# Decode states read in place, B projected second, and the group norm one projection later in a hybrid pool/SSD trunk

## The chip, the core and the metric

The kernel runs on one core of a Trainium2 chip. The metric is the time of one execution on the device, in microseconds (us). Below, PE is TensorE (matmuls), PEld its weight loads, DVE is VectorE, ACT ScalarE, POOL GpSimd, and SP the engine whose queue issues the weight loads. All inputs and outputs are in the chip's main memory, and everything counts that the program does between its first and its last instruction.

## The reference

One layer of a streaming encoder is run for 256 new frames of one stream (the prompt) and 16 frames of each of 8 running streams (the sample), 384 columns in all, which share the weights. The input is normed and projected by `w_in`; the projection's columns are split into a pooling branch, z, xBC, dt and gates. The part that matters here is the state-space branch (SSD): 8 groups, each with 8 heads of 64 channels, one B and one C of 128 states.

```
xbc, new_conv = causal_conv(xbc, st_conv, p['conv_w'], p['conv_b'])   # 4 taps, SiLU
...
def step(h, inp):
    ...
    cb = jnp.einsum('btgn,bsgn->btsg', Cc, Bc)
    xdt = xc * dtc[..., None]
    y = jnp.einsum('btsgr,bsgrp->btgrp', cb[..., None] * decay, xdt)
    y = y + jnp.einsum('btgn,bgrpn->btgrp', Cc, h) * jnp.exp(cum)[..., None]
    last = cum[:, -1]
    w_end = jnp.exp(last[:, None] - cum)
    h = h * jnp.exp(last)[..., None, None] + jnp.einsum('bsgn,bsgr,bsgrp->bgrpn', Bc, w_end, xdt)
    return h, y
...
y = y + p['d_skip'].astype(jnp.float32).reshape(SSD_GROUPS, HEADS_PER_GROUP)[..., None] * xh
a_ssd = gated_rmsnorm(y.reshape(b, L, D_INNER), z, p['ssd_norm']).astype(u.dtype)
```

`gated_rmsnorm` multiplies y by silu(z) and norms it over each group of 512 channels. For the sample, every stream has 16 frames, so its new state h is its old one times a decay, plus the product of B and the weighted x over its own 16 frames. This last product, for 8 streams at once, is what the kernel calls `su`. The pooling branch, the gates, the two branch projections, `w_out`, and an MLP of 8192 channels with its norms follow the same input and make up the rest of the time.

## The kernel before

All matmuls of the projections are made of three passes of a reduced fp32 kind: each operand is split into a high part (a rounded copy) and a low part (the rest), and high times high, high times low and low times high are summed (`mm3`, lines 98 to 100). Weights are streamed in pieces of 512 KB, half a projection each: SP's queue loads a piece (`wfetch`, line 63), ACT copies the high part (`wh`, line 70), DVE subtracts it for the low part (`wl`, line 71). There are three buffers of each, and `take` keeps three split halves ahead of TensorE.

The part that the change touches is the loop over the groups, from about 418 to 1180 us. In each of its passes TensorE runs ten projections of 128 channels, each of two halves of 24 matmuls over 384 columns: x0, x1, B, C, x2, x3 and then z0 to z3. Two lumps of small matmuls stand between them. One comes in the middle, after x2, and finishes the second pair of heads of the group before (`prev`): its prompt states `t_pp` (line 696), then `t_cb` (line 652, C times B of the new group), `t_yT` and `t_Y` (line 682, the outputs), `t_yi` (line 661) and `t_su` (line 820). The other comes at the end, after z3, and does the same, without `t_cb`, for the first pair of the group itself; the profile has the first rows of both lumps as `py L696`.

What feeds them: `conv` (four taps and SiLU) on DVE and ACT makes x, B and C; `turned` turns x and B over (a transpose in blocks on DVE, four POOL DMAs to the scratch t_scr, a fifth that loads it back as xT or Bt). `xside` makes xdt and splits the weighted x into `xhl`; `bside` splits Bt into `Bhl`; `eside` makes the decay matrices E (Relu and Exp on ACT, a product with `cbm` on DVE); `dside` multiplies the loaded states hs with their decay. Work that consists of several DMAs is laid out over half projections by `steps` and `tick`.

For `t_su`, frames of the 8 streams lie on 128 partitions, 16 each. A stream's own 16 rows are not a unit that TensorE can address, so the low and the high half of B and x are stacked: b_scr and x_scr are written out and read back by 16 rows at a time (`leave` and `come`, lines 714 to 719 and 765 to 774) as `bst` and `xst`, each with 64 rows for one stream.

After the lump `final` adds the D skip, multiplies with z, squares (`ysq`, line 857 on ACT) and sums the squares into `ssum` (line 858 on POOL). `finish` is the group norm of the group before: `norm_bc` copies ssum's high part (`nh`, line 192, ACT), subtracts (`nl`, line 193, DVE), sums over partitions by two matmuls with ones (`bc_g`, lines 196 and 197), and `newton` (lines 182 to 186, DVE) takes the inverse root. Then DVE multiplies the four tiles zs (line 865), and POOL writes them out to a_scr. In the code `finish(prev)` stands ahead of `zproj(2)`.

A scheduler orders each engine's instructions once, when the program is built; on the chip each engine and each queue works in that order and waits at the instruction whose inputs are missing. Two kinds of functions on ACT, Silu on one side and Exp on the other, need different tables, and each switch is an ACT_TABLE_LOAD.

## Time and profile before

| what | value |
|---|---|
| median of 3 runs | 2664.36 us (2659.24 to 2667.16) |
| the profiled execution's own time | 2661.4 us |
| its span, first to last instruction | 2659.6 us |
| PE busy | 2638.4 us |
| DVE, ACT, POOL busy | 1521.6, 1169.5, 379.4 us |
| mean granted TensorE clock | 0.996 |
| main memory read, written | 414.97 MB, 49.58 MB |

The busy times say how long each engine had an instruction running. TensorE's matmuls are pipelined, so that a matmul's shown duration (0.33 us in the projections) is about twice the distance to the next one (0.16 us). The chain of work that ended last is followed backwards from the last instruction, at each step to what released it. Where TensorE waits for nothing, the chain runs along TensorE alone; where another engine or a DMA stands in it, TensorE had to wait, and the lines ahead of such a place show for what. A row of the chain has its start, its length and what it is. A row of waits has the engine and line that waited, what it waited for, and the total, the number and the longest of these waits in us.

### The profile page before, as it was taken

The numbers are of one execution on the slowest core, as the hardware profiler recorded it, in microseconds if no ns is written. First come the engines' busy times: TensorE is split into PE (matmuls) and PEld (weight loads), VectorE is DVE, ScalarE is ACT, GpSimd is POOL, SyncE is SP. The second block draws the span as 40 slices with busy tenths as digits, with TensorE's granted clock in tenths as the row PEclk, the third lists the DMA queues.
The fourth block names the chain that finished last, engine by engine and source line by source line (L and its number), as shares of the span: only waits on it lengthen the run. The fifth ranks groups of instructions, "written<-read, shape, count | busy, mean of one in ns | idle before, by whom it ended". The sixth has DMA issues, their size and how long they took to land.

```text
span 2659.6 us, 38491 instructions
## 1 busy us (share of the span) xinstructions
PE 2638.4 (99%) x15149; PEld 2457.0 (92%) x15149; DVE 1521.6 (57%) x2148; ACT 1169.5 (44%) x1820; POOL 379.4 (14%) x550
## 2 busy tenths in 40 slices
PE   9999999999999999999999999999999999999998
PEld 8998889999999999988888889999999999989897
DVE  7585335788888879756344346534444444444446
ACT  6443225566566757545322235433333333323233
POOL 0000002355454453530000000000000000000000
PEclk9999999999999999999999999999999999999999
DMA  7544446677777677767544544444444444444443
GB/s 273 154 134 152 147 148 232 202 232 225 244 240 240 227 237 248 222 213 250 173 158 151 189 162 136 139 138 137 136 135 135 135 135 135 135 135 136 136 137 130
DMA packets 144117, 467.09 MB, mean 176 GB/s; under 512 B 20864, under 2 KB 35776, under 8 KB 138944
## 3 DMA queue, kind: packets, MB, share of 16 engines
q1 hardware_dynamic: 112000, 365.76, 41.8%
q0 software_dynamic: 25024, 84.19, 9.4%
q10 hardware_dynamic: 6912, 14.68, 1.8%
q8 instruction: 119, 1.95, 0.3%
q14 instruction: 62, 0.51, 0.1%
HBM read 414.97 MB, written 49.58 MB: 175 GB/s over the span
## 4 chain that ended last, share of the span: by engine, by line
PE 93%; DVE 2%; ACT 2%; DMA 2%; issue 1%; POOL 0%; SPq 0%; DVEq 0%; ACTq 0%; POOLq 0%
PE pj_up L98 6%; PE pj_up L100 6%; PE pj_up L99 6%; PE wd L151 6%; PE wd L149 6%; PE wd L150 6%; PE pj_x L98 4%; PE pj_x L99 4%; PE pj_x L100 4%; PE pj_sp L150 3%; PE pj_sp L149 3%; PE pj_sp L151 3%; PE pj_z L100 3%; PE pj_z L99 3%; PE pj_z L98 3%; PE pj_gb L149 2%
## 5 line engine op out<-in xcount | busy, mean ns | idle before, releaser
L98 PE MATMUL pj_up<-x1h,wh_up 128*128 128x384 f32 (+1 forms) x1024 | 333.7, 326 | 0.0
L99 PE MATMUL pj_up<-x1l,wh_up 128*128 128x384 f32 (+1 forms) x1024 | 333.4, 326 | 0.0
L100 PE MATMUL pj_up<-x1h,wl_up 128*128 128x384 f32 (+1 forms) x1024 | 333.4, 326 | 0.0
L71 DVE TENSOR_TENSOR wl_wd<-w_wd,wh_wd 128x1024 fp32r<-128x1024 f32 x126 | 154.4, 1225 | 240.3 <-ACT wh_wd L70 240.3
L149 PE MATMUL wd<-wh_wd,hh 128*128 128x512 f32 x756 | 286.5, 379 | 0.0
L150 PE MATMUL wd<-wl_wd,hh 128*128 128x512 f32 x756 | 286.5, 379 | 0.0
L151 PE MATMUL wd<-wh_wd,hl 128*128 128x512 f32 x756 | 286.5, 379 | 0.0
L70 ACT ACTIVATE wh_wd<-w_wd 128x1024 fp32r<-128x1024 f32 x126 | 133.1, 1057 | 322.2 <-PE wd L151 261.7
L70 ACT ACTIVATE wh_up<-w_up 128x1024 fp32r<-128x1024 f32 x126 | 133.1, 1057 | 292.8 <-PE pj_up L99 229.4
L71 DVE TENSOR_TENSOR wl_up<-w_up,wh_up 128x1024 fp32r<-128x1024 f32 x126 | 154.4, 1225 | 178.8 <-ACT wh_up L70 178.5
L98 PE MATMUL pj_x<-xgh,wh_x 128*128 128x384 f32 x768 | 251.9, 328 | 0.0
L99 PE MATMUL pj_x<-xgl,wh_x 128*128 128x384 f32 x768 | 250.4, 326 | 0.0
L100 PE MATMUL pj_x<-xgh,wl_x 128*128 128x384 f32 x768 | 250.4, 326 | 0.0
L99 PEld LDWEIGHTS pj_up<-x1l,wh_up 128*128 128x128 f32 x1024 | 193.6, 189 | 0.2
L98 PEld LDWEIGHTS pj_up<-x1h,wh_up 128*128 128x128 f32 x1024 | 193.6, 189 | 0.2
L100 PEld LDWEIGHTS pj_up<-x1h,wl_up 128*128 128x128 f32 x1024 | 193.6, 189 | 0.0
L98 PE MATMUL pj_z<-xgh,wh_z 128*128 128x384 f32 x512 | 170.0, 332 | 1.9 <-ACT wh_z L70 1.9
L100 PE MATMUL pj_z<-xgh,wl_z 128*128 128x384 f32 x512 | 170.2, 332 | 0.9 <-DVE wl_z L71 0.9
L99 PE MATMUL pj_z<-xgl,wh_z 128*128 128x384 f32 x512 | 169.9, 332 | 0.0
L71 DVE TENSOR_TENSOR wl_sp<-w_sp,wh_sp 128x1024 fp32r<-128x1024 f32 x64 | 78.4, 1225 | 154.0 <-ACT wh_sp L70 154.0
L151 PEld LDWEIGHTS wd<-wh_wd,hl 128*128 128x128 f32 x756 | 142.9, 189 | 20.3
L150 PEld LDWEIGHTS wd<-wl_wd,hh 128*128 128x128 f32 x756 | 142.9, 189 | 20.1
(336 smaller groups left out, 6119.3 us busy)
## 6 DMA issues: line engine op xcount, KB each, us to landing
w_up<-w_up SPq DMA_DIRECT2D x128, 512.0 KB, 3.3
w_wd<-w_down SPq DMA_DIRECT2D x128, 512.0 KB, 3.3
w_x<-w_in SPq DMA_DIRECT2D x96, 512.0 KB, 4.6
w_z<-w_in SPq DMA_DIRECT2D x64, 512.0 KB, 4.1
w_sp<-w_ssd SPq DMA_DIRECT2D x64, 512.0 KB, 3.3
w_ga<-w_ga SPq DMA_DIRECT2D x32, 512.0 KB, 3.4
w_pp<-w_pp SPq DMA_DIRECT2D x32, 512.0 KB, 3.3
hs<-ssm POOLq DMA_DIRECT2D x16, 1024.0 KB, 6.9
```

The source lines that it names most:

```text
L70: cut[0] = s.activation(h, w, AF.Copy)
L71: cut[1] = v.tensor_tensor(l, w, h.bitcast(F32), ALU.subtract)
L98: te.matmul(out, wh, xh, start=first, stop=False, **how)
L99: te.matmul(out, wh, xl, start=False, stop=False, **how)
L100: return te.matmul(out, wl, xh, start=False, stop=last, **how)
L149: te.matmul(out, mh, vh, start=k == 0, stop=False)
L150: te.matmul(out, mh, vl, start=False, stop=False)
L151: last[0] = te.matmul(out, ml, vh, start=False, stop=k == nk - 1)
```

## The change

The states of the streams are computed from `xhl` and B where they lie. `t_su` uses row tiles of 32 partitions, two streams each. To keep two streams apart, B is multiplied beforehand with a mask that is one on the 16 rows of the even (or odd) streams and zero on the others (`Bm`, two ACT copies with a scale per partition, the mask in two new columns of `vec`). There are then 4 row tiles, 2 parities and 3 passes of high and low parts, 24 matmuls instead of 8, in four PSUM tiles at once. The scratch tensors b_scr and x_scr, the tiles bst and xst, and all their DMAs are gone.

The order of the projections is x0, B, x1, C, x2, x3, with the weights stored accordingly. `finish(prev)` stands behind `zproj(2)`. The tiles zs have 8 buffers instead of 7, and ysq two instead of one.

```
@@
-        bst = []
-        for i in range(2):
-            bst.append(pd1.tile([P, 4, P], F32R, name=f"bst{i}"))
@@ def bside(D)
-            bscr = b_scr[D.g]
-            D.bs = bst[D.g % 2]
-
-            def leave():
-                gp.dma_start(bscr, D.Bhl[:, :, 2, :].bitcast(F32))
-
-            def come():
-                for p4 in range(4):
-                    for h2 in range(2):
-                        gp.dma_start(
-                            D.bs[h2 * 64 + p4 * 16 : h2 * 64 + p4 * 16 + 16].bitcast(F32),
-                            bscr.rearrange("(q h r) l n -> h l r q n", q=4, h=2)[h2, p4 // 2],
-                        )
-
-            steps.append([leave] + [lambda: None] * 2 + [come])
+            D.Bm = pd.tile([P, 2, 2, P], F32R, tag="Bm", name=f"Bm{D.g}", bufs=1)
+            for h in range(2):
+                s.activation(
+                    D.Bm[:, h],
+                    D.Bhl[:, :, 2, :].bitcast(F32),
+                    AF.Copy,
+                    scale=vec[:, V_PAR + h : V_PAR + h + 1],
+                )
@@ def xside(S)
-            xscr = x_scr[S.qd]
-            def leave():
-                sy.dma_start(
...
-            def come():
-                S.xst = pd.tile([P, 4, 2 * P], F32R, tag="xst", name=f"xst{S.nm}", bufs=1)
-                for p4 in range(4):
-                    for h2 in range(2):
-                        gp.dma_start(
...
-            if S.qd == 2 * G - 1:
-                leave()
-                come()
-            else:
-                steps.append([leave] + [lambda: None] * 3 + [come])
@@ def state(S), t_su
-                for r2 in (0, 2):
-                    su = [sstile(f"su{S.nm}_{r2}_{h}") for h in range(2)]
-                    for r in range(2):
-                        for h in range(2):
-                            t = slice(h * 64, h * 64 + 64)
+                su = [sstile(f"su{S.nm}_{q}") for q in range(4)]
+                for h in range(2):
+                    for n, (bl, xl) in enumerate(((0, 0), (0, 1), (1, 0))):
+                        for q in range(4):
+                            t = slice(q * 32, q * 32 + 32)
                             i = te.matmul(
-                                pairs(su[h][:, r * 256 : r * 256 + 256]),
-                                S.D.bs[t, r2 + r, :],
-                                woven(S.xst[t, r2 + r, :]),
-                                start=True,
-                                stop=True,
+                                pairs(su[q][:, h * 256 : h * 256 + 256]),
+                                S.D.Bm[t, h, bl, :],
+                                S.xhl[t, xl, :, 2, :].rearrange("p j n -> p n j"),
+                                start=n == 0,
+                                stop=n == 2,
                             )
@@ def final(S)
-                    qs = pd.tile([P, T], F32, tag="ysq", name=f"ysq{g}_{j}", bufs=1)
+                    qs = pd.tile([P, T], F32, tag="ysq", name=f"ysq{g}_{j}")
@@ the loop
-            cs = [g * 4, g * 4 + 1, 32 + g, 40 + g, g * 4 + 2, g * 4 + 3]
+            cs = [g * 4, 32 + g, g * 4 + 1, 40 + g, g * 4 + 2, g * 4 + 3]
@@
-                z = pd.tile([P, T], F32, tag="zs", name=f"zs{g}_{j}", bufs=7)
+                z = pd.tile([P, T], F32, tag="zs", name=f"zs{g}_{j}", bufs=8)
@@
+            zproj(2)
             if g:
                 finish(prev)
-            zproj(2)
             dside(S)
             zproj(3)
```

How the orders differ at the places that matter is shown for group 4 and its turn to group 5. First TensorE, where the projections of z follow each other. Before, the norm's two matmuls stand between z1 and z2:

```order
L98 MATMUL pj_z_1_8397<-xgh_514,wh_z_1_1_8348 128x384
L99 MATMUL pj_z_1_8397<-xgl_515,wh_z_1_1_8348 128x384
L100 MATMUL pj_z_1_8397<-xgh_514,wl_z_1_1_8349 128x384
L196 MATMUL bc_g_8489<-nh_g_8485,onesr 128x384
L197 MATMUL bc_g_8489<-nl_g_8486,onesr 128x384
L98 MATMUL pj_z_2_8513<-xgh_250,wh_z_2_0_8400 128x384
L99 MATMUL pj_z_2_8513<-xgl_251,wh_z_2_0_8400 128x384
```

Now, between z2 and z3:

```order
L98 MATMUL pj_z_2_8467<-xgh_490,wh_z_2_1_8433 128x384
L99 MATMUL pj_z_2_8467<-xgl_491,wh_z_2_1_8433 128x384
L100 MATMUL pj_z_2_8467<-xgh_490,wl_z_2_1_8434 128x384
L196 MATMUL bc_g_8535<-nh_g_8531,onesr 128x384
L197 MATMUL bc_g_8535<-nl_g_8532,onesr 128x384
L98 MATMUL pj_z_3_8560<-xgh_226,wh_z_3_0_8470 128x384
```

The norm has moved by a whole projection on TensorE.

Next ACT, from the split of z1's second half (wh_z_1_1) to that of z2's first (wh_z_2_0). L792, L790, L800 and L801 make E, L601 is the SiLU of a conv, L954 that of z0, nh_g is the norm's copy, the DMA rows load the decays for E. Before:

```order
L70 ACTIVATE wh_z_1_1_8348<-w_z_1_1_8346 128x1024
L792 ACTIVATE E_0_8298<-cbc_0_1_7874,tok 128x128 x3
L800 ACTIVATE E_0_8298<-E_0_8298 128x2x128
L801 ACTIVATE E_0_8298<-E_0_8298 128x2x256
L646 DMA cbc_1_0_8393<-cum_scr 128x768
L601 ACT_TABLE_LOAD
L601 ACTIVATE xs_8293<-cacc_8288,vec 128x384
L954 ACTIVATE zs_0_8379<-zs_0_8379 128x384
L646 DMA cbc_1_1_8395<-cum_scr 128x768
L70 ACTIVATE wh_z_2_0_8400<-w_z_2_0_8398 128x1024
L70 ACTIVATE wh_z_2_1_8443<-w_z_2_1_8441 128x1024
L192 ACTIVATE nh_g_8485<-ssum_7682 128x384
```

Now (L758, L756, L766 and L767 make E, L596 is the conv's SiLU, L919 that of z0):

```order
L758 ACTIVATE E_0_8298<-cbc_0_1_7866,tok 128x128 x3
L766 ACTIVATE E_0_8298<-E_0_8298 128x2x128
L70 ACTIVATE wh_z_1_1_8347<-w_z_1_1_8345 128x1024
L596 ACT_TABLE_LOAD
L596 ACTIVATE xs_8290<-cacc_8285,vec 128x384
L767 ACT_TABLE_LOAD
L767 ACTIVATE E_0_8298<-E_0_8298 128x2x256
L641 DMA cbc_1_0_8392<-cum_scr 128x768
L919 ACT_TABLE_LOAD
L919 ACTIVATE zs_0_8378<-zs_0_8378 128x384
L641 DMA cbc_1_1_8394<-cum_scr 128x768
L70 ACTIVATE wh_z_2_0_8399<-w_z_2_0_8397 128x1024
```

The part of E that stood behind wh_z_1_1 has moved ahead of it, and between the two splits there are three table loads instead of one.

Last DVE, around the end lump, before from the last of the norm's four multiplications on: wl_x is the low half of the x and B weights (x_0 and x_1 are the halves of a projection; the last one in the second pair of lists is the second half of the second projection), L953 and L918 multiply the projection of z, L865 and L830 are the norm's multiplications of zs, L844 and L809 the D skip, L852 and L817 the product with z, L829 and L794 the addition of su, L753 and L741 make xdt and weight xT.

```order
L865 SCALAR_TENSOR_TENSOR zs_3_7614<-zs_3_7614,vec,ny_g_8494 128x384
L71 TENSOR_TENSOR wl_x_0_8582<-w_x_0_8579,wh_x_0_8581 128x1024
L71 TENSOR_TENSOR wl_x_1_8612<-w_x_1_8609,wh_x_1_8611 128x1024
L953 TENSOR_TENSOR zs_3_8639<-pj_z_3_8578,rstd 128x384
L71 TENSOR_TENSOR wl_x_0_8720<-w_x_0_8717,wh_x_0_8719 128x1024
L844 SCALAR_TENSOR_TENSOR xs_7762<-xs_7762,vec,Y_0_0_8649 128x384
L852 TENSOR_TENSOR zs_0_8379<-zs_0_8379,xs_7762 128x384
L844 SCALAR_TENSOR_TENSOR xs_7859<-xs_7859,vec,Y_0_1_8651 128x384
L753 TENSOR_TENSOR xdt_1_8789<-xT_1_8218,tok 128x384
L741 TENSOR_TENSOR yis_1_8685<-py_1_8642,tok 128x256
L829 TENSOR_TENSOR hs_0_7957<-hs_0_7957,su_0_0_0_8687 128x2x256
L829 TENSOR_TENSOR hs_0_7957<-hs_0_7957,su_0_0_1_8688 128x2x256
```

Now, from z3's own multiplication on:

```order
L918 TENSOR_TENSOR zs_3_8621<-pj_z_3_8560,rstd 128x384
L830 SCALAR_TENSOR_TENSOR zs_0_7347<-zs_0_7347,vec,ny_g_8540 128x384
L830 SCALAR_TENSOR_TENSOR zs_1_7431<-zs_1_7431,vec,ny_g_8540 128x384
L830 SCALAR_TENSOR_TENSOR zs_2_7497<-zs_2_7497,vec,ny_g_8540 128x384
L830 SCALAR_TENSOR_TENSOR zs_3_7590<-zs_3_7590,vec,ny_g_8540 128x384
L809 SCALAR_TENSOR_TENSOR xs_7754<-xs_7754,vec,Y_0_0_8631 128x384
L809 SCALAR_TENSOR_TENSOR xs_7950<-xs_7950,vec,Y_0_1_8633 128x384
L817 TENSOR_TENSOR zs_0_8378<-zs_0_8378,xs_7754 128x384
L729 TENSOR_TENSOR yis_1_8667<-py_1_8624,tok 128x256
L817 TENSOR_TENSOR zs_1_8462<-zs_1_8462,xs_7950 128x384
L71 TENSOR_TENSOR wl_x_0_8718<-w_x_0_8715,wh_x_0_8717 128x1024
L741 TENSOR_TENSOR xdt_1_8787<-xT_1_8216,tok 128x384
```

And the rows ahead of the second half's split itself, before:

```order
L852 TENSOR_TENSOR zs_1_8480<-zs_1_8480,xs_7859 128x384
L753 TENSOR_TENSOR xT_1_8218<-xT_1_8218,tok 128x384
L753 TENSOR_TENSOR xdt_1_8789<-xT_1_8218,tok 128x384
L805 TENSOR_TENSOR hs_1_8483<-hs_1_8483,decb 128x2048
L71 TENSOR_TENSOR wl_x_1_8750<-w_x_1_8747,wh_x_1_8749 128x1024
L753 TENSOR_TENSOR xT_1_8218<-xT_1_8218,tok 128x384
L802 TENSOR_TENSOR E_1_8798<-E_1_8798,cbm_8169 128x1024
```

and now:

```order
L741 TENSOR_TENSOR xT_1_8216<-xT_1_8216,tok 128x384
L741 TENSOR_TENSOR xdt_1_8787<-xT_1_8216,tok 128x384
L768 TENSOR_TENSOR E_1_8796<-E_1_8796,cbm_8151 128x1024
L741 TENSOR_TENSOR xT_1_8216<-xT_1_8216,tok 128x384
L771 TENSOR_TENSOR hs_1_8465<-hs_1_8465,decb 128x2048
L71 TENSOR_TENSOR wl_x_1_8748<-w_x_1_8745,wh_x_1_8747 128x1024
L749 TENSOR_TENSOR xhl_1_8792<-xT_1_8216,xhl_1_8792 128x768
```

The four multiplications of zs have moved behind the multiplication of z3 (L953, L918), the first half's split from ahead of the D skip to behind the products with z, and the E product and a second xT product (L753, L741) from behind the second half's split to ahead of it.

More of the change, by code (lines that the diff above doesn't have):

```diff
@@ L30 @@
 C_RC, C_SCAN, C_END = 1032, 1096, 1504
-V_GPRE, V_GMLP, V_PSC, V_CW, V_CB, V_NRM, V_DSK, V_DTB, V_ALOG, V_END = 0, 16, 32, 48, 240, 288, 320, 352, 353, 384
+V_GPRE, V_GMLP, V_PSC, V_CW, V_CB, V_NRM, V_DSK, V_DTB, V_ALOG, V_PAR, V_END = 0, 16, 32, 48, 240, 288, 320, 352, 353, 354, 384
 def build(ctx, tc, io):
@@ L206, in build @@
     gb_scr = [dram.tile([P, 3, 512], F32, name=f"gb_scr{i}") for i in range(4)]
-    b_scr = [dram.tile([P, 2, P], F32, name=f"b_scr{i}") for i in range(G)]
-    x_scr = [dram.tile([P, 2, 2, P], F32, name=f"x_scr{i}") for i in range(16)]
     t_scr = [dram.tile([T, P], F32, name=f"t_scr{i}") for i in range(40)]
@@ L912, in build @@
                 eside(prev.p[1], 0)
-            D.xs.append(conv(u0 + 1, g * 4 + 1, "xs", 6))
-            xturned(D, g, 1)
+            D.BT = conv(u0 + 1, 32 + g, "BT", 2)
+            D.Bt = pd.tile([P, 3, P], F32, tag="Bt", name=f"Bt{g}", bufs=1)
+            turned(D.BT, 32 + g, D.Bt)
             if g:
@@ L917, in build @@
             cload(D.p[0])
-            D.BT = conv(u0 + 2, 32 + g, "BT", 2)
-            D.Bt = pd.tile([P, 3, P], F32, tag="Bt", name=f"Bt{g}", bufs=1)
-            turned(D.BT, 32 + g, D.Bt)
+            D.xs.append(conv(u0 + 2, g * 4 + 1, "xs", 6))
+            xturned(D, g, 1)
             pload(D.p[0])
@@ L1421 @@
     for g in range(G):
-        cols += [6144 + (g * 4 + j) * P for j in range(2)]
-        cols += [6144 + 4096 + g * P, 6144 + 5120 + g * P]
+        cols += [6144 + g * 4 * P, 6144 + 4096 + g * P, 6144 + (g * 4 + 1) * P, 6144 + 5120 + g * P]
         cols += [6144 + (g * 4 + j) * P for j in range(2, 4)]
@@ L1437 @@
     vec[:NH, V_ALOG] = a["a_log"][0]
+    for h in range(2):
+        vec[:, V_PAR + h] = (np.arange(P) // TS_) % 2 == h
     d = {
```

13 lines of the change are left out of this document (3 added, 10 removed).

## The prediction

> **What bounds the kernel now.** I read the busy times first, then the chain that ended last, then the waits of the engine that carries it.
>
> ```profile
> PE 2638.4 (99%) x15149; PEld 2457.0 (92%) x15149; DVE 1521.6 (57%) x2148; ACT 1169.5 (44%) x1820; POOL 379.4 (14%) x550
> ...
> PE 93%; DVE 2%; ACT 2%; DMA 2%; issue 1%; POOL 0%; SPq 0%; DVEq 0%; ACTq 0%; POOLq 0%
> ```
>
> TensorE is the bound. The change can win only by closing holes in its work (the 7% of the chain that is not PE), and lose by adding matmuls or opening new holes. All removed DMAs and scalar work count at nothing unless they stand ahead of such a hole. So the next view is the waits of TensorE (us in total, times, longest):
>
> ```profile
> PE bc_g L196 <- ACT nh_g L192: 3.6, 2, 2.0
> PE bc_g L197 <- DVE nl_g L193: 2.7, 3, 0.9
> PE pj_z L98 <- ACT wh_z L70: 1.9, 1, 1.9
> ...
> PE cb L652 <- ACT xs L601: 0.9, 1, 0.9
> ```
>
> Nearly all lies in the loop over eight groups, and most of it at the group norm's broadcast matmuls (bc_g), the step that the change moves. How much time that costs is read from the chain, in which every pass of the loop shows the first matmuls of its two lumps of small matmuls (start, us):
>
> ```profile
> 499.85 0.67 PE py L696 x6
> ...
> 589.41 0.67 PE py L696 x6
> ...
> 632.90 0.67 PE py L696 x6
> ...
> 678.34 0.67 PE py L696 x6
> ...
> 772.70 0.67 PE py L696 x6
> ...
> 816.20 0.67 PE py L696 x6
> ...
> 820.73 0.64 PE su L820 x8
> ...
> 860.90 0.67 PE py L696 x6
> ...
> 864.56 0.64 PE su L820 x8
> ...
> 904.40 0.67 PE py L696 x6
> ...
> 953.73 0.67 PE py L696 x6
> ...
> 1041.93 0.67 PE py L696 x6
> ...
> 1136.61 0.67 PE py L696 x6
> ```
>
> The rows alternate between the lump in a group's middle and the one at its end. From an end to the next middle it is 43.50 (772.70 to 816.20, 860.90 to 904.40), from a middle to its end 44.70 (816.20 to 860.90), a whole group 88.20. Against that, group 1 (499.85 to 589.41) has 1.36 too much, the second half of group 2 (632.90 to 678.34) 0.74, group 3 (678.34 to 772.70) 6.16, the second half of group 5 (904.40 to 953.73) 4.63, group 7 (1041.93 to 1136.61) 6.48. Sum 19.4 us. With the 0.9 that the first group's cb matmuls wait, the loop holds about 20.3 us of loss. Its mechanism in group 7, in the chain:
>
> ```profile
> 1104.95 9.68 DMA w_z<-w_in
> ...
> 1114.71 1.06 ACT wh_z L70
> ...
> 1117.55 0.69 PE bc_g L197
> 1118.23 0.32 PE pj_z L98
> ```
>
> The DMA part of the page has the usual landing beside it (KB each, median us):
>
> ```profile
> w_z<-w_in SPq DMA_DIRECT2D x64, 512.0 KB, 4.1
> ```
>
> So a weight load takes 9.68 us where 4.1 is usual, its split wh_z stands on ScalarE ahead of the norm's copy nh, and TensorE waits at bc_g although the weights that come behind bc_g would be there in time. Then each projection matmul advances by 0.32 instead of 0.16 us: the granted clock has fallen, as the stretches show (stretch, length, busy times, clock, DMA share, GB/s):
>
> ```profile
> 816.00:861.00 45.00, 45.00 (x333) 43.80 (x332) 39.88 (x61) 29.37 (x54) 22.71 (x36) 1.00 0.74 240
> 1085.40:1136.60 51.20, 48.29 (x331) 46.56 (x330) 39.93 (x60) 29.02 (x52) 27.68 (x37) 0.93 0.69 222
> ```
>
> A clock of 0.93 over 51.2 us is 3.6 us, so a hole of some 2 to 3 us costs as much again in clock; the wait of 0.9 at cb is not followed by such matmuls. The Trainium skill ("TensorE: Matmul & The Clock Gate", section "Why this matters for your kernels") allows holes up to about 3 us before the clock halves; this trace halves it after less, so the rows decide. By the page, the price of rival C below would be 7 x 2.2 = 15 us, and it would end at 2663 instead.
>
> Group 3 has another cause:
>
> ```profile
> 730.30 6.04 POOL ssum L858
> ...
> 739.85 0.96 ACT wh_z L70
> ...
> 742.11 0.69 PE pj_z L100
> 742.80 0.32 PE pj_z L98
> ```
>
> ScalarE's second square ysq has one buffer and must wait until GpSimd's addition (6.04 us here) has read the first one; behind it on ScalarE stands the split of z0's second half, for which TensorE waits at 740.
>
> **The change, part by part.**
>
> Norm one projection later, and second ysq buffer. bc_g now stands between z2 and z3, 7.8 us later, while nh stands on ScalarE right behind the split of z2's second half, which TensorE wants 3.9 us earlier than bc_g. In groups 5 and 7 nh was 2.0 late at most: 7.8 covers it. The price is that newton and the four multiplications of zs fall 7.8 us later on VectorE, at the group's end (below). With two ysq buffers group 3's wait is gone. I take all 20.3; the bounds are 14 (group 3's 6.2 stays, from the GpSimd addition or another cause) and 20.3.
>
> States. Before, 8 matmuls of 64 rows, in four rounds of two tiles side by side:
>
> ```profile
> L820 PE MATMUL su<-xst,bst x128: 272/272/374, 503.4 to 1175.3; 64*128 64x256 f32 x128
> ...
> 1045.52 0.71 PE L820 MATMUL su<-xst,bst 64*128 64x256 f32 x8
> ```
>
> 0.71 is the first round's 0.374 and three more of 0.112. Now 24 matmuls of 32 rows, with as many columns. If four tiles run side by side, these are six rounds: 2 x 0.112 = 0.22 more, x16 pairs = +3.6 us, all on TensorE. No row shows four row tiles at once. If only two run together, it is 12 rounds, 0.90 more, +14.3 in all; if none do, 24 rounds, 2.24 more, +36. It cannot be under four rounds. I take +3.6, nearest to the su row, where tiles do run together and the rounds go by columns. The four sums need four PSUM banks at once instead of two and two; VectorE adds the same four halves of hs (L829), so that side costs nothing.
>
> Scratch trips. SP loses 16 x_scr issues, which wait long:
>
> ```profile
> SPq L765 <- DVE xhl L761: 118.4, 16, 16.5
> ```
>
> and the weight loads queue behind them, while GpSimd's queue loses 25 issues per group (16 xst, 8 bst, b_scr). The turned x3, the state load hs and a_scr now start sooner there. I count no gain of its own: where TensorE did not wait, these were hidden. The hs load (1024 KB), however, now always stands early, ahead of the late z weights, as it did before only in groups 1, 3, 5 and 7; that is rival E. The two Bm copies (128x256) cost ScalarE less each than the 0.53 of the 128x384 zs row below, at the beginning of a group's second half, and are wanted only by the su at its end, 35 us later: nothing.
>
> B second. x1's turned tile arrives a projection later, and is first read by VectorE in the second half of the group; Bt has more time than before, which frees ScalarE's Bhl. No cost on TensorE; in the first group the cb wait goes with it.
>
> New tight places. The scheduler's order on ScalarE now switches between Silu and Exp three times between the splits of z1's and z2's halves, where there was one such load:
>
> ```profile
> 837.52 1.28 ACT L601 ACT_TABLE_LOAD   x1
> ...
> 840.18 0.53 ACT L954 ACTIVATE zs<-zs 128x384 f32<-128x384 f32 x1 [0.74 <-DVE zs L953]
> 840.61 2.10 ACT L70 ACTIVATE wh_z<-w_z 128x1024 fp32r<-128x1024 f32 x2
> ```
>
> Two loads more are 2.6, less about half of the 0.74 that was idle: z2's first split ends near 843.8 instead of 841.7, VectorE's half of it 1.2 later, 845.0. TensorE wants it at 821.37 + six half projections of 3.9 + the odd tenths, 845.1, and the low half 0.33 later. Some 0.3 are left of 2.5. The other place is behind the end lump on VectorE:
>
> ```profile
> 856.00 2.20 DVE L865 SCALAR_TENSOR_TENSOR zs<-zs,vec,ny_g 128x384 f32<-128x384 f32 x4
> ...
> 872.32 1.22 DVE L71 TENSOR_TENSOR wl_x<-w_x,wh_x 128x1024 fp32r<-128x1024 f32 x1
> 873.46 0.55 DVE L753 TENSOR_TENSOR xT<-xT,tok 128x384 f32<-128x384 f32 x1
> 873.92 1.22 DVE L802 TENSOR_TENSOR E<-E,cbm 128x1024 f32<-128x1024 f32 x1
> ```
>
> The second row is the low half for the second projection's second half, done at 873.5, wanted at 865.20 (the end of the su row at 864.56) + 3 half projections of 3.9 + 0.33 = 877.2, and now 0.2 later for the longer su. The four multiplications (2.1) now come after z3's own, so all behind them comes later, and in the new order the E product (1.2) and the xT product (0.5), which stood behind that split in this group, stand ahead of it: 873.5 + 2.1 + 1.2 + 0.5 = 877.3 against 877.4, nothing to spare. Seven groups, two places, each between 0 and 0.8 late: I take the middle, 0.36 x 14 = +5; the ends are 0 and +11.
>
> Sum against the profile's own time of 2661.4 (span 2659.6): 2661.4 - 20.3 + 3.6 + 5 = 2649.7. The median of the runs, 2664.4, lies 3.0 above it, so 2652.7, say 2652. Ends: 2648 with no new wait, 2659 with all of them, 2665 if group 3's loss stays as well.
>
> **The rivals** (on the median's scale; 0.3%, 8 us, is what this kernel's measurement can tell from nothing, so 2656.4 to 2672.4 is no change).
>
> B. The tight places miss by about 1 us each, under the size that drops the clock: 14 x 1.0 in place of 5, giving 2662. For it: the slack of 0.3 and 0.1 rests on hand sums over ten instructions. Against: both sums assume no overlap beyond what the rows show.
>
> C, the slower one. At z2 ScalarE misses by over 2 us in each of the seven groups. From there the clock falls too and each miss costs what group 3 lost, 6.2: 2648 + 7 x 6.2 = 2691. It decides from about 2.3 later than my 843.8, that is two table loads more or a zs that waits long. For it: the orders of groups 1 to 6 are alike, so one miss is seven. Against: nothing in the order adds two.
>
> D. Row tiles do not run four together: two at a time 2652 + 10.7 = 2663, one at a time 2652 + 32 = 2684. Against the latter: the su row's pairs.
>
> E. The change doesn't do what it says: late weights, not the norm's place, make the holes. The 9.68 load stands for it; with hs early in each group, holes like the 1.9 of pj_z stay in three or four groups at some 4 to 5 us: 2652 + 16 = 2668. Against: the small packets of xst and bst that shared the queues then are gone, and in group 7 the split itself was in time for z2.
>
> **How the numbers follow.** Forecast 0.56, with its own range 2645 to 2660; B 0.22; C 0.08; D 0.06 (half of it one at a time); E 0.08. Faster: nine tenths of the forecast and a little of B, 0.53. Slower: C, the bad half of D and a little of E, 0.13. Same: the rest, 0.34. The range from 2644 to 2670 leaves out C, the bad D, a third of E and the forecast's low tail, below 2 in 10.
>
> **What would show it.** Groups of 88.2 + 0.44 between like lumps in the chain, and no PE wait at bc_g; no 0.32 steps among the z matmuls; su as x24 at about 0.87; 14 table loads more. The first waits to look for are pj_z on wl_z or wh_z at z2's first half and pj_x on wl_x at the second projection. I am wrong if these show above 1 us a time, if su takes 1.6 or more, or if w_z landings of 9 us stand ahead of holes.

## The result, and the profile after

The changed kernel takes 2667.4 us (median of 20 runs, 2664.6 to 2668.8). The kernel before, run beside it, takes 2665.8 us (20 runs, 2659.2 to 2670.3). The ratio is 1.0007, with a 95% interval of 1.0000 to 1.0014: no difference by the measure of 0.3%. The forecast was 2652 us and faster.

The head of the page after, and its chain by engine:

```profile
PE 2639.9 (99%) x15405; PEld 2454.2 (92%) x15405; DVE 1528.4 (57%) x2148; ACT 1196.3 (45%) x1850; POOL 226.6 (9%) x350
...
PE 74%; issue 14%; DVE 7%; ACT 3%; DMA 1%; POOL 1%; DVEq 0%; ACTq 0%; POOLq 0%
```

GpSimd lost 40% of its work (379.4 to 226.6 us), and the time did not follow it. The waits of TensorE:

```profile
PE pj_z L100 <- DVE wl_z L71: 5.6, 9, 0.7
PE pj_gb L149 <- DVE hs L794: 3.8, 2, 2.1
PE cb L647 <- ACT xs L596: 1.5, 1, 1.5
...
PE pj_gb L150 <- DVE wl_gb L71: 0.9, 1, 0.9
```

Both rows of bc_g are gone. In their place stand short waits at the z weights, two at the first matmuls of the gate behind the loop (pj_gb, for the additions of su to hs), and one at cb that is longer than before. The lumps at the groups' ends, from the chain:

```profile
509.29 0.87 PE su L785 x24
...
1049.38 0.87 PE su L785 x24
```

A group now takes 90.0 us, the same in all seven ((1049.38 - 509.29) / 6), where undisturbed groups took 88.20. The profiled spans, 2664.6 and 2659.6, differ by 5.0 us, and the account closes when first and last starts of the same tiles are set against each other in both traces:

| stretch | what moved there | us |
|---|---|---|
| before the loop | a late start at the beginning, no part of the change | +1.25 |
| group 0 | new loss | +4.5 |
| groups 1 to 7 | old stalls gone, -19.4; 7 x 1.82 new | -6.6 |
| the gate behind the loop, and the last su | new loss | +5.9 |

The 1.82 of a group are 0.46 of su (two pairs), 0.37 at z0's second half and 0.99 at z2's first. So there are three new losses, of 4.5 us in group 0, 7 x 1.36 = 9.5 in the groups behind it (su's own 0.46 left aside) and 5.9 at the gate, and only the one in the middle is of a kind that the prediction spoke of.

**Group 0.** The chain of after ahead of the first conv:

```profile
420.65 5.23 DMA ma_scr<-sg
...
427.10 6.09 DMA cstate<-state_conv
...
433.42 1.05 ACT wh_x L70
```

GpSimd's timeline, before:

```profile
419.93 0.54 POOL L562 DMA_DIRECT2D cstate<-state_conv  x1
```

and after:

```profile
427.10 0.54 POOL L560 DMA_DIRECT2D cstate<-state_conv  x1 [5.92 <-ACT E L756]
```

The load of the conv states (cstate) was issued behind three writes of ma_scr without a wait; now it waits until the data of the last write have left (420.65 + 5.23 = 425.9; the E named in brackets only ended nearest to it). ACT's first conv copy starts 5.3 us later (433.30 in place of 427.99; 1.25 of it is the late start), and wh_x stands behind that copy. In the kernel the pool of the loop's tiles has become 1 KB per partition larger (xst out; Bm, the eighth zs and the second ysq in), and cstate, first in the small pool behind it, now lies where sg lay, the gate tile that is still being written out to ma_scr.

**z2.** ACT's timeline in group 4, from z1's split to z2's:

```profile
841.76 1.28 ACT L596 ACT_TABLE_LOAD   x1
...
843.69 1.28 ACT L767 ACT_TABLE_LOAD   x1
...
845.63 1.28 ACT L919 ACT_TABLE_LOAD   x1
...
847.36 1.99 ACT L70 ACTIVATE wh_z<-w_z 128x1024 fp32r<-128x1024 f32 x2
```

These are the three loads that the order showed. z2's first half of the split ends at 848.4, DVE's low half of it 1.2 later, and TensorE, which reaches z2 at 848.5, wants the low half with its third matmul: 0.67 of waiting there, 0.99 lost over the half projection.

**The gate.** DVE's timeline behind the last group:

```profile
1136.87 2.19 DVE L830 SCALAR_TENSOR_TENSOR zs<-zs,vec,ny_g 128x384 f32<-128x384 f32 x4
...
1141.30 1.01 DVE L741 TENSOR_TENSOR xdt<-xT,tok 128x384 f32<-128x384 f32 x2
...
1143.18 2.47 DVE L794 TENSOR_TENSOR hs<-hs,su 128x512 f32<-128x512 f32 x4
```

and TensorE's, with what it waited for in brackets:

```profile
1139.35 0.94 PE L785 MATMUL su<-xhl,Bm 32*128 32x256 f32 x24
...
1143.91 0.48 PE L149 MATMUL pj_gb<-wh_gb,xgh 128*128 128x512 f32 x1 [2.12 <-DVE hs L794]
```

The gate's third PSUM tile takes the bank of su's first tile, and that is free only when the first addition of hs has read it. The four additions cost 2.47 as before, but stand behind xdt and xT now, and start 3.8 us after the start of su, where it was 0.9 in the kernel before.

### The profile page after: what moved, and what is told of

It is laid out like the page before. It is cut to its first block, busy times and chain, and to the rows that moved or that the text cites. A ratio compares the mean times of both kernels' runs of the same rounds, so it can differ in the third digit from the quotient of the medians.

```text
span 2664.6 us, 38740 instructions
## 1 busy us (share of the span) xinstructions
PE 2639.9 (99%) x15405; PEld 2454.2 (92%) x15405; DVE 1528.4 (57%) x2148; ACT 1196.3 (45%) x1850; POOL 226.6 (9%) x350
## 4 chain that ended last, share of the span: by engine, by line
PE 74%; issue 14%; DVE 7%; ACT 3%; DMA 1%; POOL 1%; DVEq 0%; ACTq 0%; POOLq 0%
PE pj_up L98 6%; PE pj_up L100 6%; PE pj_up L99 6%; PE wd L151 6%; PE wd L150 6%; PE wd L149 6%; PE pj_x L98 3%; PE pj_x L99 3%; PE pj_x L100 3%; PE pj_sp L150 3%; PE pj_sp L149 3%; PE pj_sp L151 3%; PE pj_z L100 2%; PE wo L151 2%; PE wo L149 2%
## 5 line engine op out<-in xcount | busy, mean ns | idle before, releaser
L149 PEld LDWEIGHTS wd<-wh_wd,hh 128*128 128x128 f32 x756 | 142.9, 189 | 20.1
```

Source lines behind the costliest of these rows:

```text
L149: te.matmul(out, mh, vh, start=k == 0, stop=False)
```

## The experiments

The theory from here on: the change clears the stalls it was to clear, and gives the gain back at three places that have nothing to do with its arithmetic, namely where a tile lies in memory (group 0) and where the scheduler, which sees another number of su matmuls, puts the hs additions (the gate) and the Exp of E (z2). The rivals are that the removed or moved work itself does it: the norm's new place, B's new place, the second ysq buffer, or the cost of the row tiles.

**e1, another place for ysq.** The loop's pool gets back below its old size.

```
-                    qs = pd.tile([P, T], F32, tag="ysq", name=f"ysq{g}_{j}")
+                    qs = pd1.tile([P, T], F32, tag="ysq", name=f"ysq{g}_{j}", bufs=2)
```

> The changed kernel with one thing different: the two ysq buffers come from the small pool behind the loop's big one, so that the conv states' tile no longer lies on the memory of the gate tile sg, whose last write to main memory lands about 5 us after the loop's start. Theory A (memory placement makes group 0 late): the load of the conv states is issued about 5.9 us sooner, group 0 loses its 4.5 us against the kernel before, the time falls by 4 to 5 us to about 2663; the later groups stay at about 90.0 us each. Rival (B projected second makes group 0 late): group 0 stays as it is, no change above 1 us.

Measured: 2663.15 us, ratio to before 1.0005 (0.9996 to 1.0014), and 4.1 us under e3 below, which ran on the same chip with the same group length as the changed kernel. GpSimd's timeline:

```profile
421.38 0.55 POOL L560 DMA_DIRECT2D cstate<-state_conv  x1
```

No wait stands at the load, the wait at cb falls from 1.5 to 0.3, and group 0, from its first projection to the next group's, takes 87.0 us in place of 90.6. The waits at z and at pj_gb stay. Of group 0's new loss of 4.5 us, 3.6 are a tile's place; what the rest is wasn't tried.

**e2, the second pairs' E ahead of z0**, to take its Exp from between the splits.

```
+            eside(S, 1)
             zproj(0)
-            eside(S, 1)
```

> The changed kernel with the second half of the decay matrices (eside for the second head pair) issued ahead of z0's projection instead of behind it; ScalarE then has 55 table loads instead of 69, and none between the splits of z1's and z2's last and first halves. Theory A (the two more table loads make z2's first half late by 1.0 us in each of seven groups): that wait goes, 7 us less, about 2660, if VectorE's E product, which comes earlier too, doesn't make z0's or z1's halves late instead; then a wait of up to 1 us stands there and the gain is 0 to 4. Rival (VectorE, not ScalarE, is late at z2): no change of the wait at z2.

Measured: 2674.3 us, 1.0050 (1.0038 to 1.0063): slower. The table loads fell, and z2 was in time, but the Exps and E's product on DVE now stand ahead of z1's splits:

```profile
PE pj_z L100 <- DVE wl_z L71: 7.7, 9, 1.2
PE pj_z L98 <- ACT wh_z L70: 4.0, 7, 0.6
```

A group takes 91.0. The wait moved a projection forward and grew. The expectation was missed; a place for the Exp alone is not the remedy.

**e3, the hs additions held ahead of the second z product and of xdt.** `behind(x)` tells the scheduler to keep an instruction behind x.

```
-                v.tensor_tensor(z, z, x, ALU.mult)
+                with behind(added[0] if q else None):
+                    v.tensor_tensor(z, z, x, ALU.mult)
@@ state, t_su
-                    v.tensor_tensor(hr, hr, su[q].rearrange("p (h n a) -> p h a n", h=2, a=2), ALU.add)
+                    added[0] = v.tensor_tensor(hr, hr, su[q].rearrange("p (h n a) -> p h a n", h=2, a=2), ALU.add)
```

The products for xdt get the same `behind`.

> The changed kernel with VectorE's order held so that the four additions of su to hs come ahead of the second product with z and of the xdt products. Theory A (behind the loop the gate's third PSUM tile waits for a bank that su held, because these additions come late on VectorE): the two waits of the gate's matmuls for hs, 3.8 us in all, fall to under 1 us, the split behind them is in time, 3 to 5 us less, about 2663; the groups themselves stay within 0.5 us each. Rival (four su tiles at once take the bank, whatever VectorE's order): the waits stay.

Measured: 2667.3 us, 1.0021 (1.0012 to 1.0031); the expectation was missed. DVE's timeline at the gate shows why nothing was won:

```profile
1141.95 2.28 DVE L773 TENSOR_TENSOR hs<-hs,decb 128x2048 f32<-128x2048 f32 x1
1144.15 2.47 DVE L796 TENSOR_TENSOR hs<-hs,su 128x512 f32<-128x512 f32 x4
```

The scheduler filled the place with the decay of the next states. The additions start 5.3 us after su, later than the 3.8 of the changed kernel, so this run says nothing on the theory.

**e4, the norm back ahead of z2**, the rest as changed.

```
-            zproj(2)
             if g:
                 finish(prev)
+            zproj(2)
```

> The changed kernel with the group norm put back ahead of z2's projection; all else as changed. Theory A (the two more table loads make all of ScalarE's work behind z1 late, and nh stands behind both splits of z2): TensorE waits at bc_g about 2.8 us in each of seven groups instead of 1.0 at z2, and the clock falls behind most of these, 5 to 6 us a group; less 3 us behind the loop, where VectorE has less to do. 2685 to 2705. Rival (the scratch trips alone made the norm late): without them the norm is in time, no wait at bc_g, and the time is 2660 to 2668.

Measured: 2680.4 us, 1.0073 (1.0061 to 1.0086), less slow than expected.

```profile
PE bc_g L196 <- ACT nh_g L192: 8.0, 7, 1.2
PE bc_g L197 <- DVE nl_g L193: 5.3, 7, 0.8
PE pj_gb L149 <- DVE hs L794: 3.7, 2, 2.1
```

In this order the norm's wait returns in all seven groups, so its move does clear it. The gate's wait for hs is the same with the norm's four multiplications out of the way: they were not its cause. Its wait of 0.9 for a split (pj_gb on wl_gb) is gone in this order, though, so that one is a price of the norm's later place.

**e5, the additions held ahead**: e1 and e3 together, with the decay of the states and, behind the loop, the splits of the gate's weights held behind them too.

```
         cut[0] = s.activation(h, w, AF.Copy)
-        cut[1] = v.tensor_tensor(l, w, h.bitcast(F32), ALU.subtract)
+        with behind(ahead[0]):
+            cut[1] = v.tensor_tensor(l, w, h.bitcast(F32), ALU.subtract)
@@ dside
-            v.tensor_tensor(
+            with behind(added[0]):
+                v.tensor_tensor(
...
@@ behind the loop
                 state(prev.p[1])
+                ahead[0] = added[0]
```

> The kernel of e1 (conv states placed well), with VectorE's four additions of su to hs held ahead of the second product with z, of the xdt products, of the decay of the other pair's states, and, behind the loop, of the gate's weight splits. With this order the scheduler also puts one table load instead of three between the splits of z1's last and z2's first half (55 loads in all, as before the change). Theory A: z2's wait of 1.0 in seven groups goes, and of the 3.8 at the gate's third bank at least half; z0's 0.4 stays or goes. 8 to 12 us less than e1. Rival (z2's wait is VectorE's or the bank is held by the number of su tiles): less than 3 us.

Measured: 2649.1 us (2648.5 to 2650.0), 0.9939 (0.9926 to 0.9952). It beats both kernels. Its waits and its chain:

```profile
PE pj_z L102 <- DVE wl_z L73: 1.2, 2, 0.8
...
PE pj_gb L151 <- DVE hs L799: 0.9, 1, 0.9
```

```profile
594.97 0.87 PE su L790 x24
...
772.29 0.87 PE su L790 x24
```

A group takes 88.66 ((772.29 - 594.97) / 2), which is 88.20 and two pairs of su at 0.23 more; the prediction had named 88.64 as its sign. Against e1, the loop gains 7 x 1.37 and the gate 4.2, more than the 8 to 12 expected. And z2's wait went, though nothing was done to the Exp. The loop's table loads, grouped by line, in the changed kernel (total and mean ns of one behind the bar):

```profile
L756 ACT ACT_TABLE_LOAD x24 | 30.8, 1283 | 0.3
...
L767 ACT ACT_TABLE_LOAD x7 | 9.0, 1283 | 0.1
L919 ACT ACT_TABLE_LOAD x7 | 9.0, 1283 | 0.1
```

With a row of 24 at L596 these are 62. e5 has two rows of 24 and no other. So both extra loads of a group came with the place of the additions on DVE, through the scheduler.

**e6, one ysq buffer**, the rest as changed (`bufs=1`).

> The changed kernel with one ysq buffer again (the conv states then lie well too, so it is compared with e1). Theory A (with two buffers GpSimd's two additions to ssum run back to back while VectorE works, which took 1.36 for a conv step of 0.61 and 1.82 for two products of 1.02; that makes z0's second half 0.35 to 0.4 late): the wait at z0 goes, 2 to 3 us less than e1. Rival (ScalarE waits for the buffer again, as in group 3 before the change): z0's or z1's halves late by 1 us or more, 5 to 15 us more than e1.

Measured: 2662.9 us, 0.9994 (0.9985 to 1.0002), as e1: here too the pool falls below its old size. Groups of 90.0 and z0's loss of 0.38 stay, though GpSimd's two additions no longer stand back to back, so the expectation was missed: DVE's steps beside them are still slowed (1.34 for a product of 0.55, and 1.82 for the pair for xdt, which took 1.02 in the kernel before). The second buffer is needed for nothing here.

**e7, the norm's move alone, in the kernel before** (with eight zs; ysq in the small pool makes the room).

```
+            zproj(2)
             if g:
                 finish(prev)
-            zproj(2)
```

> The kernel before with the group norm behind z2's projection and eight zs buffers, and nothing else (its one ysq buffer is moved to the small pool so that the conv states lie as before). Theory A (the norm's place alone removes the waits at bc_g): the excess of groups 1, 5 and 7, 12.5 us, goes; group 3's 6.2, which comes from the ysq buffer, stays; VectorE at the group's end costs nothing to 3 us. 9 to 13 us less than before. Rival (the weights themselves come late): the same groups show waits of pj_z for wh_z of 1 us or more instead, less than 4 us gained.

Measured: 2659.7 us (2650.8 to 2669.1), 0.9986 (0.9973 to 1.0000).

```profile
PE pj_z L100 <- DVE wl_z L71: 4.7, 2, 2.5
PE pj_gb L150 <- DVE wl_gb L71: 3.2, 1, 3.2
...
PE pj_z L98 <- ACT wh_z L70: 1.8, 1, 1.8
```

The waits at bc_g are gone, and groups 1, 2, 3, 5 and 6 take 88.20. But groups 4 and 7 still lose 2.5 and 7.4 us at z0's weights, so the move clears only a part of the 19.4, and the stretch behind the loop takes 5.3 us longer than before, with the 3.2 at a split of the gate's weights in it. What makes z0 late is seen on ACT, in group 7 of this run and in group 3 of the kernel before:

```profile
1085.74 0.52 ACT L708 ACTIVATE Bhl<-Bt 128x384 fp32r<-128x384 f32 x1 [7.55 <-DMA Bt<-t_scr]
```

```profile
727.57 0.52 ACT L708 ACTIVATE Bhl<-Bt 128x384 fp32r<-128x384 f32 x1 [4.02 <-DMA Bt<-t_scr]
```

ACT waits for the turned B, and the splits of z0 stand behind that copy. In group 7 no wait for the ysq buffer follows; in the kernel before one of 3.60 does.

**e8, B third again**, the rest as changed.

```
-            cs = [g * 4, 32 + g, g * 4 + 1, 40 + g, g * 4 + 2, g * 4 + 3]
+            cs = [g * 4, g * 4 + 1, 32 + g, 40 + g, g * 4 + 2, g * 4 + 3]
```

> The changed kernel with B projected third again. Theory A (B's place moves no bound): groups 1 to 7 within 0.3 us each of 90.0, group 0 within 2 us; in all within 3 us of the changed kernel. Rival (B second is what frees ScalarE from waiting for Bt, and Bt third makes it late): waits of 1 us or more at z0's second half in groups 1 to 7, 7 us or more on top.

Measured: 2664.1 us (2657.9 to 2668.8), 0.9998 (0.9986 to 1.0009). The profiled run is the shortest of the ten; in it group 1 takes 90.0, but groups 2 to 7 take 88.8 to 89.1, and their waits at z are nearly gone. The expectation was missed in that run, and what the longer ones did isn't known. But the one trace holds both cases, with all 62 table loads and with the additions of hs behind xdt in each. DVE and GpSimd in group 1:

```profile
552.74 1.00 POOL L823 TENSOR_TENSOR ssum<-ssum,ysq 128x384 f32<-128x384 f32 x1 [6.92 <-ACT ysq L822]
...
552.81 1.35 DVE L817 TENSOR_TENSOR zs<-zs,xs 128x384 f32<-128x384 f32 x1
```

and in group 4:

```profile
821.45 1.02 DVE L741 TENSOR_TENSOR xdt<-xT,tok 128x384 f32<-128x384 f32 x2
...
821.64 2.80 POOL L823 TENSOR_TENSOR ssum<-ssum,ysq 128x384 f32<-128x384 f32 x2 [5.46 <-ACT ysq L822]
```

In group 1 GpSimd's addition starts first, and DVE's product takes 1.35 in place of 0.55, its pair for xdt later 1.82 in place of 1.02; in groups 2 to 7 ACT waits 2.1 to 2.5 us for the turned B, GpSimd starts later, when DVE's pair is under way, and DVE is not slowed. So the waits at z stand where GpSimd slows DVE, and the table loads alone don't make them.

**e9, su with a third of its matmuls** (only high times high), on e1.

```
-                    for n, (bl, xl) in enumerate(((0, 0), (0, 1), (1, 0))):
+                    for n, (bl, xl) in enumerate(((0, 0),)):
```

> The kernel of e1 with only the pass of high parts in the states' product: 8 matmuls instead of 24, so the small parts of B and x are left out of the streams' new states. Nothing else is edited, but with 8 matmuls the scheduler puts VectorE's additions of su right behind the products with z, and ScalarE's table loads are 55 again, one between the splits of z1 and z2. Theory A (the 24 matmuls cost twice: 0.22 per pair on TensorE, and more by the orders that the scheduler makes of them): su takes 0.49 instead of 0.87, 6 us less in all, and the waits at z0 and z2 go (10 us) and part of the gate's: 2643 to 2648. Rival (the waits have nothing to do with the number of matmuls): the waits stay, only 6 us less than e1, 2655 to 2659.

Measured: 2645.3 us, 0.9929 (0.9916 to 0.9943). A pair of su takes 0.42 in place of 0.87, which is worth 16 x 0.45 = 7.2 of the 17.2 us to e1 by the profiled spans (2661.3 and 2644.1). The rest is order. DVE's, at the end lump of group 4, in e1:

```
L817 TENSOR_TENSOR zs_1_8462<-zs_1_8462,xs_7950 128x384
L71 TENSOR_TENSOR wl_x_0_8718<-w_x_0_8715,wh_x_0_8717 128x1024
L741 TENSOR_TENSOR xdt_1_8787<-xT_1_8216,tok 128x384
L794 TENSOR_TENSOR hs_0_7952<-hs_0_7952,su_0_0_8669 128x512
```

and in e9:

```
L817 TENSOR_TENSOR zs_1_8334<-zs_1_8334,xs_7838 128x384
L794 TENSOR_TENSOR hs_0_7840<-hs_0_7840,su_0_0_8541 128x512
...
L71 TENSOR_TENSOR wl_x_0_8574<-w_x_0_8571,wh_x_0_8573 128x1024
L741 TENSOR_TENSOR xdt_1_8643<-xT_1_8088,tok 128x384 x2
```

Groups take 87.76, exactly 88.20 less two times 0.22, and the wait at the gate for hs is 0.7 in place of 3.8 (one of 2.8 for a split of its weights has come instead, and the stretch behind the loop is only 0.6 shorter than in e1, less than su's own 0.9). Nothing but the number of matmuls differs in the code, so that number sets the place of the additions, and with it most of z's waits (0.9 us in all here, 5.7 in e1).

**e10 and e11, e5 with the norm back ahead of z2, and e5 with B third** (the edits of e4 and e8).

> The kernel of e5 (additions of su held ahead) with the group norm put back ahead of z2's projection. Theory A (with ScalarE's order mended and the scratch traffic gone, nh and nl are ready about 1 us before TensorE comes to bc_g, by e5's trace): no wait at bc_g above 0.3 us, groups 1 to 7 at 88.7, the time within 2 us of e5, so the norm's move is worth nothing there. Rival (the norm's move is what removes the waits at bc_g): waits of 1 us or more in several groups, 7 to 20 us more than e5.

> The kernel of e5 with B projected third again. Theory A (B's place is worth nothing once VectorE's order is held): groups 1 to 7 at 88.7 to 89, group 0 within 2 us, the time within 3 us of e5. Rival (Bt comes too late for ScalarE's Bhl, ahead of z0's splits, as in group 3 before the change): waits at z0's second half of 1 us or more in some groups, 5 us or more on top, and times that vary from run to run.

Measured: 2649.0 us, 0.9942 (0.9928 to 0.9955), and 2650.5 us, 0.9946 (0.9931 to 0.9962), both the same as e5. Groups take 88.66 in both, and no wait at bc_g returns in e10. Only group 0 differs: cb waits 0.3 us in e5, 1.7 in e10 and 2.0 in e11, and the group takes 87.2, 87.5 and 89.2, so that B's place is worth 2 us at most. With the order held, neither move is worth anything that can be told. Since the second ysq buffer is worth nothing either (e6, and e12 below), what e5 gains over the kernel before is left to the states read in place; the three were taken away one at a time, not together, and B second alone in the kernel before was not run.

**e12, the second ysq buffer alone, in the kernel before** (ysq in the small pool, two buffers).

> The kernel before with two ysq buffers (in the small pool, the conv states lie well), nothing else. Theory A (group 3's loss is ScalarE's wait for the buffer that GpSimd's addition holds): no loss of 2 us or more at z0 in any group, the waits at bc_g stay: 4 to 7 us less than before. Rival (Bt's late landing alone makes ScalarE late there): a loss of 4 to 7 us at z0's second half stays in one or two groups, less than 2 us gained.

Measured: 2663.4 us (2656.3 to 2669.1), 0.9999 (0.9988 to 1.0011).

```profile
PE bc_g L196 <- ACT nh_g L192: 9.5, 4, 2.9
...
PE pj_z L100 <- DVE wl_z L71: 1.4, 1, 1.4
```

Nothing is gained by the medians. Group 3 has no wait at z0 in this run, but loses 6.5 us all the same, at bc_g now, and group 4 loses 1.8, most of it at z0's weights, behind a wait of 4.38 for the turned B and none for the buffer. So the buffer does not win the 6.2 us that the prediction gave it, and expectation and rival were each right in part. The course of such a kernel differs from run to run, and this is one run.

## Why the prediction was wrong

**The stalls that go: right in size, in part wrong in cause.** All 19.4 us of the profiled run's groups 1 to 7 went. But the norm's place and ysq's buffer don't account for them as the prediction has it. The norm's move does clear the waits at bc_g (e7), but leaves z0's losses. Those begin with ACT's wait for the turned B, 4.02 us in group 3 and 7.55 in e7's group 7, and the prediction's reading of group 3 names only the 3.60 behind it, for the buffer; the buffer alone gains nothing (e12) and isn't needed (e6). With B second ACT waits for the turned B in none of groups 1 to 7. And once the scratch trips are gone and the order is held, B can stand third (e11) and the norm where it stood (e10). "I count no gain of its own" was the wrong line on the scratch trips: with their 25 issues per group off GpSimd's queue and the issues that waited up to 16.5 us off SP's, the longest landing of a z weight falls from 10.4 us to 7.6. That the trips made the weights late is by elimination and not by a run of its own. Over the loop (416 to 1182 us) GpSimd's busy time falls from 352.8 to 198.5 us and the DMA share from 0.71 to 0.62; which of the two queues mattered wasn't tried.

**The row tiles: right.** The su row is 0.87 us, 0.23 longer than 0.64, where 0.22 was predicted; four tiles run side by side, and rival D falls.

**The tight places: the right kind, mis-sized.** z2's first half loses 0.99 us a group, not 0.36, rival B's size; z0's second half, not named, loses 0.37; and the second projection's second half, given 0.36, loses nothing. Together 9.5 us in place of 5. The cause is seen in the trace. DVE of the changed kernel in group 4:

```profile
822.04 0.61 DVE L592 SCALAR_TENSOR_TENSOR cacc<-cbuf,vec,cacc 128x384 f32<-128x384 f32 x1
...
825.41 1.36 DVE L592 SCALAR_TENSOR_TENSOR cacc<-cbuf,vec,cacc 128x384 f32<-128x384 f32 x1
826.69 1.82 DVE L741 TENSOR_TENSOR xdt<-xT,tok 128x384 f32<-128x384 f32 x2
```

and GpSimd:

```profile
824.88 2.75 POOL L823 TENSOR_TENSOR ssum<-ssum,ysq 128x384 f32<-128x384 f32 x2 [4.09 <-ACT ysq L822]
```

While GpSimd adds, DVE's operations take up to twice as long (0.61 to 1.36, and 1.82 for a pair that took 1.02 before), 1.5 us in all, and z0's low half stands behind them. ACT in turn stands idle for 1.31 us until DVE's products with xT are done, and its splits of z1 and z2 come later by about 1 us than in e8's undisturbed groups, which uses up the slack that the prediction found for the two table loads. The slack itself was summed about rightly: in e8's groups 2 to 7, where DVE isn't slowed, z2 passes with all three loads, and a group loses 0.15 to 0.45 us against 88.66.

**The failed step** is this one: "VectorE adds the same four halves of hs (L829), so that side costs nothing." The durations are the same, 2.47 us for four. Their place isn't: with 24 matmuls in su the scheduler puts them behind xdt, and at the gate behind xT too. That keeps a PSUM bank from the gate: of its 5.9 us, 3.8 are waits for it (0.9 are the split's, from the norm's later place, 0.5 are su itself, and 0.7 no row of waits names). And it shifts what follows on DVE and ACT in every group: where the additions stood when GpSimd begins to add, operations stand now that GpSimd slows. e5 (the additions held) takes away the groups' 1.37 us each and 4.2 at the gate; e9 (fewer matmuls, nothing else) takes away the groups' too, but at the gate trades the wait for one at a split. The order of the changed kernel showed the place of the additions; I read from it who stands behind the four multiplications of zs, and not who waits for a bank that su's tiles hold.

**Not in the working at all:** where tiles lie. 1 KB more in one pool cost 3.6 us once, in group 0 (e1; 3.4 by e6's 87.3). "In the first group the cb wait goes" fails by the same cause: it grew from 0.9 to 1.5, and is 0.3 in e1.

**Rivals.** C did not come (its point was 2.3 us of lateness at z2; it was 1). E did not come either: w_z lands after 4.5 us (median), and no hole behind a late landing is left in the loop. But its doubt about the norm's place was in part sound: in e10 the norm stands where it did, and no wait returns. B was right on z2 and still not the answer. e5 takes 2649.1, near the sum's 2652, but that is in part luck: its groups lose nothing at the tight places, for which the sum has 5, and group 0 and the gate still lose some that the sum doesn't have.

## What to carry to other kernels

When a change alters how many instructions a step issues, compare the scheduler's order of everything that releases that step's buffers (PSUM banks above all) and follow who takes the buffer next, also behind the end of the loop, and what comes to stand beside another engine's work. When pool sizes change, look at the first load into each tile that sits behind the pool: if the memory under it is still being written out, the load waits for that. Holding one instruction where it stood can be worth as much as the whole change (14 us between e1 and e5).

## What the runs showed of the hardware

**The same hole costs more at one time than at another.** In e4 every group has the same two holes at bc_g (1.13 and 0.76 us of waiting, 1.5 us apart). The su rows of its chain:

```profile
509.00 0.87 PE su L785 x24
...
602.12 0.87 PE su L785 x24
...
693.55 0.87 PE su L785 x24
```

Groups take 93.1 and 91.4 us in turn (group 7 91.4 again). The stretches around the holes of groups 1 and 2 (stretch, length, busy times, clock, DMA share, GB/s):

```profile
576.00:590.00 14.00, 12.11 (x62) 11.52 (x62) 10.87 (x16) 6.25 (x10) 1.57 (x3) 0.88 0.58 195
669.00:683.00 14.00, 12.11 (x73) 11.52 (x72) 12.11 (x19) 7.36 (x11) 1.68 (x3) 1.00 0.64 206
```

0.12 of 14 us is 1.7 us, the difference of the groups. The clock fell behind the holes of groups 1, 3 and 5 and not behind those of 2, 4, 6 and 7, so the length of a hole doesn't decide alone, and the 7 x 6.2 that I gave rival C counted every hole as a lost clock. The Trainium skill ("TensorE: Matmul & The Clock Gate", "Part 1: The HAM clock gate") says that activity is judged in a free-running window of about 3.4 us; that would make the hole's place in the window decide. The trace agrees with it in kind, though the holes add up to 1.9 us only.

**DVE and GpSimd slow each other only for some operations, and it matters which starts first.** The slowed ones above have two operands in SBUF; the hs additions read one from PSUM. In e9 these stand beside GpSimd's addition, and neither is slowed:

```profile
813.60 1.00 POOL L823 TENSOR_TENSOR ssum<-ssum,ysq 128x384 f32<-128x384 f32 x1 [5.89 <-ACT ysq L822]
...
813.67 2.47 DVE L794 TENSOR_TENSOR hs<-hs,su 128x512 f32<-128x512 f32 x4
```

Where GpSimd starts when a row of DVE's operations with two SBUF operands is under way, DVE keeps its times and GpSimd takes the longer: 2.98 us for its next addition in e9, 6.04 in group 3 of the kernel before, for 1.00 when free. That is also where the prediction's 6.04 came from. The Trainium skill ("SBUF — State Buffer", "Who interferes with whom") has the first part as a rule: an operation of VectorE with two inputs in SBUF contends with a GpSimd operation that reads SBUF, and one with at most one such input, outside its 2-port modes, doesn't. The rows of cacc and xdt agree with the first half, those of e9 with the second.

**Kernels of one speed spread differently.** The runs of the kernel before cover 11 us, those of e7 and e12 18 and 13; the changed kernel's cover 4.2 and e5's 1.5. The scratch trips don't explain it, since e8, which has none, covers 10.9. What the wide ones share is B projected third: there ACT waits for the turned B in most groups, up to 7.55 us in e7, and with B second never in groups 1 to 7. That this is the reason is not shown; e11, with B third, covers 5.2 in six runs. A single profile of such a kernel is one of several courses that its waits can take.
